# Hybrid encoder, RWKV stage: both directions' chains side by side, outputs summed in PSUM, preparation and filling products dealt between them in fixed order

## The chip, the core and the metric

One Trainium2 chip, one of its cores. A core has TensorE (PE, matrix products; PEld is its weight load), VectorE (DVE), ScalarE (ACT), GpSimd (POOL) and SyncE (SP), which here issues the transfers. Each engine works through a queue of its own and waits on semaphores for the others. The metric is device time in microseconds for one launch; lower is better.

## The reference, cut to what matters

One layer of an encoder on 1024 + 256 tokens of width 1024. An input projection feeds three branches: attention over a neighbourhood of a grid (8 heads), a bidirectional RWKV-7 recurrence (8 heads of 64), and attention over 256 memory tokens (4 heads). Gates merge the branches, then follow an output projection and a feed-forward block. The recurrence is, for each direction d and head:

```python
def step(s, inp):
    r_t, w_t, k_t, v_t, a_t, b_t = inp
    sa = jnp.einsum('bhij,bhj->bhi', s, a_t)
    s = s * w_t[:, :, None, :] + sa[..., None] * b_t[:, :, None, :] + v_t[..., None] * k_t[:, :, None, :]
    return s, jnp.einsum('bhij,bhj->bhi', s, r_t)
...
for d in range(2):
    ...
    ys.append(wkv7_scan(rh, decay, k_d, vh, -kk, kk * a_h, reverse=(d == 1)))
y = ys[0] + ys[1]
```

## The kernel before, in words

Tokens lie along the free dimension. A projection of 128 columns ("block") takes 24 products for each of three token tiles of 512, 512 and 256 columns: 8 slices of the contraction times three (high weight with high input, low with high, high with low), since numbers are split into two parts. `weight_block` loads a block's weights and splits them, ScalarE the high part (`whi`), VectorE the low (`wlo`). `dense_steps` (products on line 205) yields after each 8 products; nine such steps are one block.

The stages follow one another: norms and the RWKV projections; the RWKV stage; attention of grid and memory; merge, output projection, feed-forward. The projections of grid attention (12 blocks), of memory queries (4) and of 20 of the 24 gates are not a stage: they are the **filler**, a generator from which `fill` takes steps while RWKV and attention run.

The RWKV stage (`part_rwkv`) works on 40 items: 4 pairs of heads (p), 5 groups of 256 tokens (s), 2 directions (d). An item has 4 chunks of 64 tokens.

- `rw_prepare` needs nothing of the recurrence's state. It loads k, r and kk (`kr`), makes decays (`th`, `cc`, `E2`), the left matrices `L1` and the keys `BK`, the Gram products `ps_gE` and `ps_gO` (lines 608, 611), their masked forms, and then inverts a triangular 128x128 matrix for each chunk: five doublings of `X` and `XT` (products `ps_y`, line 653, and `ps_x`, line 658; copies on ScalarE, additions and transposes on VectorE, masks `Lk` on POOL), and one correction (`ps_e`, `ps_n`). Result: `TT`, `L3`, `L1`, `R`, `wC`.
- `rw_chain` carries the state through the 4 chunks. For each chunk there are three dependent products, each followed by a copy or sum: `ps_c` from `L1` and `R` (line 707), copied to `Q`; `TT` times `Q` (line 710), copied into `R` by ScalarE and VectorE (lines 719, 720); `L3` times `R` (line 722), from which VectorE makes the next state (731, 732) and the output `Ys` (733, 734, with a part of `Q` added). The tile `ps_c` has one buffer.

Each item is written as: preparation, some filler steps, the chain of the item before, more filler steps. That is only a priority: a scheduler deals instructions to the engines' queues by readiness as it models it. Elsewhere (feed-forward) the kernel pins PE, DVE, ACT and POOL to the written order by `in_order`.

In attention, `grid_attention` runs 80 tiles of 128 queries (scores `ps_s`, softmax, transposes `ps_pt`, output `ps_o`, ended by line 946 on ScalarE), `memory_attention` 20 pairs of tiles; after each of these 100 pieces it takes `self.steps` filler steps. How many is set in lines 844 and 845:

```python
            self.fill(FILL_FIRST)
            self.steps = (9.0 * (16 + RWKV_GATES + ATTENTION_GATES) - self.filled) / 100 * FILL_ATTENTION
```

`self.filled` counts the steps taken since the start of the RWKV stage; FILL_FIRST is 40, FILL_ATTENTION 0.9. `rw_finish` turns the RWKV output round by 64x64 products with the identity (`ps_yt`, line 1058).

Of the kernel before, what the change touches and what calls it, by code (L numbers as in the profile page):

```python
# [30 lines left out]
FILL_PREPARE, FILL_ALL, FILL_FIRST, FILL_ATTENTION = 0.475, 0.955, 40, 0.9  # L31
# [46 lines left out]
def make_consts():  # L78
# [3 lines left out]
    c["ident16"] = np.eye(128, dtype=np.float16)  # L82
    hb = np.arange(128) // 64
# [71 lines left out]
class Builder:  # L155
# [195 lines left out]
    def rwkv_consts(self):  # L351
# [15 lines left out]
        self.ident16 = ld("ident16", [128, 128], F16)  # L367
        d0 = ld("rw_decay0", [128, 2, 4])
# [135 lines left out]
    def part_rwkv(self):  # L504
        nc, tc = self.nc, self.tc
        with ExitStack() as cx:
            pool = cx.enter_context(self.pool("rw", 2))
            self.psg = cx.enter_context(self.pool("psg", 2, space=PSUM))
            self.psl = cx.enter_context(self.pool("psl", 1, space=PSUM))
            self.psi = cx.enter_context(self.pool("psi", 1, space=PSUM))  # L510
            self.psc = cx.enter_context(self.pool("psc", 1, space=PSUM))
            self.L1 = [pool.tile([128, 4, 2, 128], F32, name="L1_%d" % i, bufs=1) for i in range(3)]
            self.LT = [pool.tile([128, 4, 128], F32, name="LT_%d" % i, bufs=1) for i in range(2)]
            for t in self.L1 + self.LT:
                nc.gpsimd.memset(t, 0.0)
            self.item_no = 0
            fwd = [0, 1, 2, 3, 4]
            bwd = [3, 2, 1, 0, 4]
            work = []
            for p in range(4):  # L520
                for i in range(5):
                    work.append((p, 0, fwd[i]))
                    work.append((p, 1, bwd[i]))
            state = {}
            prev = None
            self.filler = chain(self.na_steps(), self.gate_steps(self.st, range(RWKV_GATES + ATTENTION_GATES)))
            self.owed, self.filled = 0.0, 0
            steps = 9.0 * (16 + RWKV_GATES) / len(work)
            for w in work:
                it = self.rw_prepare(pool, *w)  # L530
                self.fill(steps * FILL_PREPARE)
                if prev is not None:
                    self.rw_chain(pool, prev, state)
                self.fill(steps * (FILL_ALL - FILL_PREPARE))
                prev = it
            self.rw_chain(pool, prev, state)

    def rw_prepare(self, pool, p, d, s):

        nc = self.nc  # L540
        i = self.item_no
        self.item_no += 1
        L1, LT = self.L1[i % 3], self.LT[i % 2]
# [4 lines left out]
        kr = tl([128, 3, 256], "kr")  # L548
        nc.sync.dma_start(kr, self.RKV[p][s][:, 0:3, :])
        R = tl([128, 4, 2, 64], "R", bufs=3)  # L550
        nc.sync.dma_start(R, self.VR[p][:, 4 * s:4 * s + 4])

        if d == 0:
            self.lw = tl([128, 2, 256], "lw", bufs=1)
# [1143 lines left out]
```

## Time and profile before

| | |
|---|---|
| median of 3 runs | 3084.71 us (3075.01 to 3108.17) |
| the profiled execution | 3087.64 us, of which its span 3085.9 us |
| mean granted TensorE clock of the span | 0.967 |
| PE / PEld / DVE / ACT / POOL busy | 95% / 80% / 63% / 40% / 35% |
| first to last product of the chains | 391 to 1417 us |
| first transpose of a grid tile to the last of a memory tile | 1473 to 1850 us |

A PE row's duration holds its way through the array, so rows overlap; what one costs in a stream is read from start to start. A 32-bit product is two records, so a count of x4 on `ps_c` is two products. The granted clock is 1.00 at 2.4 GHz and 0.50 at 1.2 GHz.

### The profile page before, as it was taken

The numbers are of one execution on the slowest core, as the hardware profiler recorded it, in microseconds if no ns is written. First come the engines' busy times: TensorE is split into PE (matmuls) and PEld (weight loads), VectorE is DVE, ScalarE is ACT, GpSimd is POOL, SyncE is SP. The second block draws the span as 40 slices with busy tenths as digits, with TensorE's granted clock in tenths as the row PEclk, the third lists the DMA queues.
The fourth block names the chain that finished last, engine by engine and source line by source line (L and its number), as shares of the span: only waits on it lengthen the run. The fifth ranks groups of instructions, "written<-read, shape, count | busy, mean of one in ns | idle before, by whom it ended". The sixth has DMA issues, their size and how long they took to land.

```text
span 3085.9 us, 49265 instructions
## 1 busy us (share of the span) xinstructions
PE 2929.3 (95%) x18164; PEld 2477.7 (80%) x18164; DVE 1946.3 (63%) x4001; ACT 1242.3 (40%) x2693; POOL 1082.5 (35%) x1186
## 2 busy tenths in 40 slices
PE   7999989999999998999989999999899999999999
PEld 6878867767777777777877788898799999997877
DVE  6233387887887888883435551474688888883233
ACT  6322344444444544552545551022244344343232
POOL 2000166765666766662122100000245544441100
PEclk9999988997999999999979999999999999999999
DMA  6332412221222222214546534544112222245343
GB/s 229 119 120 94 137 62 67 73 78 61 76 74 70 86 64 66 66 54 132 167 123 192 178 114 157 191 163 147 66 61 71 75 77 68 68 135 165 131 146 103
DMA packets 212743, 333.51 MB, mean 108 GB/s; under 512 B 45282, under 2 KB 109538, under 8 KB 212502
## 3 DMA queue, kind: packets, MB, share of 16 engines
q1 hardware_dynamic: 211062, 325.12, 32.6%
q10 hardware_dynamic: 1440, 5.24, 0.4%
q8 instruction: 143, 2.34, 0.3%
q14 instruction: 98, 0.80, 0.1%
HBM read 230.15 MB, written 104.07 MB: 108 GB/s over the span
## 4 chain that ended last, share of the span: by engine, by line
PE 75%; DVE 10%; POOL 6%; issue 3%; ACT 3%; DMA 2%; SPq 0%; ACTq 0%; POOLq 0%; DVEq 0%
PE ps_d L205 26%; PE ps_d L1470 16%; PE ps_d L1660 9%; PE ps_w L1167 3%; PE ps_o L945 3%; PE ps_c L722 2%; PE ps_c L707 2%; PE ps_y L653 1%; PE ps_gO L611 1%; PE ps_pt L863 1%; PE ps_x L658 1%; DVE X L661 1%; PE ps_gE L608 1%; PE ps_c L710 1%; PE ps_bt L628 1%
## 5 line engine op out<-in xcount | busy, mean ns | idle before, releaser
L205 PE MATMUL ps_d<-hT,whi 128*128 128x512 f32 (+1 forms) x2688 | 689.3, 381 | 3.5 <-ACT gt L824 2.9
L205 PEld LDWEIGHTS ps_d<-hT,whi 128*128 128x128 f32 x2688 | 450.5, 194 | 65.6 <-issue 5.8
L205 PE MATMUL ps_d<-hT,wlo 128*128 128x512 f32 (+1 forms) x1344 | 358.2, 383 | 0.0
L650 POOL TENSOR_TENSOR Lk<-Lh,c_lev 128x512 f16<-128x512 f16 x200 | 242.2, 1214 | 128.2 <-PE ps_y L653 127.0
L1660 PE MATMUL ps_d<-hT,h2T 128*128 128x512 f32 x1110 | 275.4, 394 | 7.3 <-POOL hT L183 4.1
L1660 PEld LDWEIGHTS ps_d<-hT,h2T 128*128 128x128 f32 x1110 | 210.5, 190 | 54.5 <-POOL hT L183 5.3
L205 PEld LDWEIGHTS ps_d<-hT,wlo 128*128 128x128 f32 x1344 | 229.6, 197 | 29.0 <-issue 2.8
L183 DVE TENSOR_TENSOR wlo<-wraw,whi 128x512 fp32r<-128x512 f32 x152 | 117.1, 781 | 192.9 <-ACT whi L182 192.0
L1374 DVE SCALAR_TENSOR_TENSOR xk<-xk,fconv,xk 128x642 f32<-128x642 f32 (+1 forms) x176 | 178.7, 1026 | 3.1
L655 ACT CAST Yl<-ps_y 128x512 f16<-128x512 f32 x200 | 116.8, 584 | 135.6 <-PE ps_y L653 134.8
L1470 PE MATMUL ps_d<-hT,fwx 128*128 128x256 f32 (+1 forms) x1080 | 159.0, 306 | 2.2 <-ACT fwx L182 1.6
L1470 PEld LDWEIGHTS ps_d<-hT,fwx 128*128 128x128 f32 x1080 | 156.5, 188 | 2.9 <-ACT fwx L182 1.9
L660 ACT CAST X<-ps_x 128x512 f16<-128x512 f32 x200 | 116.7, 584 | 101.7 <-PE ps_x L658 95.2
L1470 PE MATMUL ps_d<-hT,fw 128*128 128x256 f32 (+1 forms) x1032 | 156.1, 310 | 0.6 <-ACT hT L182 0.6
L1340 DVE TENSOR_TENSOR xk<-ps_d,xk 128x256 f32<-128x256 f32 (+1 forms) x308 | 140.6, 480 | 22.1 <-PE ps_d L1470 21.8
L1470 PEld LDWEIGHTS ps_d<-hT,fw 128*128 128x128 f32 x1032 | 153.2, 190 | 1.6 <-ACT hT L182 0.9
L1219 POOL TENSOR_TENSOR xk<-xk 128x1536 f32<-128x1536 f32 (+1 forms) x2 | 5.8, 2918 | 387.2 <-DVE xk L1157 387.2
L182 ACT CAST whi<-wraw 128x512 fp32r<-128x512 f32 x152 | 91.3, 620 | 119.9 <-PE ps_d L205 104.8
L205 PE MATMUL ps_d<-bo,whi 128*128 128x256 f32 (+2 forms) x640 | 127.0, 337 | 4.2 <-DMA bo<-O 3.1
L1383 ACT ACTIVATE xk<-xk 128x320 f32<-128x320 f32 (+1 forms) x88 | 41.7, 474 | 214.9 <-DVE xk L1387 139.8
L707 PEld LDWEIGHTS ps_c<-R,L 128*128 128x128 f32 x640 | 92.0, 201 | 43.2 <-issue 24.8
L1470 PE MATMUL ps_d<-h2T,fw 128*128 128x384 f32 (+1 forms) x840 | 125.4, 308 | 0.0
(353 smaller groups left out, 6437.6 us busy)
## 6 DMA issues: line engine op xcount, KB each, us to landing
wraw<-in_w_in SPq DMA_DIRECT2D x112, 256.0 KB, 2.9
wraw<-in_w_up SPq DMA_DIRECT2D x88, 256.0 KB, 2.6
kr<-RKV SPq DMA_DIRECT2D x40, 384.0 KB, 3.2
bo<-O SPq DMA_DIRECT2D x24, 640.0 KB, 8.7
gate<-GT SPq DMA_DIRECT2D x20, 640.0 KB, 4.0
h2T<-AD SPq DMA_DIRECT2D x17, 704.0 KB, 3.9
h2T<-AD SPq DMA_DIRECT2D x18, 640.0 KB, 5.1
draw<-in_w_down SPq DMA_DIRECT2D x44, 256.0 KB, 2.9
```

Source lines behind the costliest of these rows:

```text
L183: (eng or nc.vector).tensor_sub(lo, src, hi.bitcast(F32))
L205: nc.tensor.matmul(ps[:, :n], lhsT=w[:, k, :], rhs=x[k][:, t0:t0 + n], start=i == 0, stop=i == 3 * kt - 1)
L650: nc.gpsimd.tensor_mul(Lk, Lh, bc(self.lev[:, d, l, :]))
L655: nc.scalar.copy(Yl, py)
L660: nc.scalar.copy(f(X2), f(px))
L707: nc.tensor.matmul(ps[:, 0, h, :], lhsT=L1[:, c, h, :], rhs=R[:, c, h, :], start=True, stop=True)
L945: nc.tensor.matmul(o, lhsT=PT[0:h, j], rhs=V[0:h, k0 // 128 + j, f], start=j == 0, stop=j == nb - 1)
L1167: nc.tensor.matmul(ps[i][:, 512 * f:512 * f + 512], lhsT=self.merged(l, k, 128 * i, 128), rhs=r[:, 512 * f:512 * f + 512], start=k == 0 an ...
L1340: add = lambda o, y: nc.vector.tensor_add(o, ps, y)
L1374: nc.vector.scalar_tensor_tensor(o[:, :m], in0=z[j][:, lo + d:lo + d + m], scalar=fc[:, f + 22 * j, i:i + 1], in1=o[:, :m], op0=ALU.mult, ...
L1470: nc.tensor.matmul(ps, lhsT=w[:, u, 128 * k:128 * k + 128], rhs=B[c][j][v][:, k], start=n == 0, stop=n == 11)
L1660: nc.tensor.matmul(ps[n], lhsT=u, rhs=wd[f][:, v], start=f == 0 and m == 0, stop=f == 21 and m == 2)
```

## The change

- Items go in pairs: chunk group s of the forward and 3-s of the backward direction (the group of the short sequence with itself). `rw_chain` carries both directions at once: 18 products for two chunks (14 where no state goes on) in place of 10, cut to 64x64 output pieces; both outputs are summed over two products each in a PSUM tile `ps_cy`, which ScalarE copies once per pair; the copies to `Q` and `R`, the state's scaling and sums take both directions in one instruction.
- The new state is written straight into the next pair's `R`; the copies through `S`, the zeroing of `R`, and VectorE's sums for `Ys` go.
- In the preparation, `ps_gE` and `ps_gO` alternate; ScalarE's copy of `ps_x` goes (VectorE adds from PSUM); VectorE's two instructions around `ps_e` become two more 16-bit products per chunk and a ScalarE copy.
- `rw_prepare` and `rw_chain` are generators. A loop deals them: 12 chain steps per pair (3 per chunk), between them the 21 steps of both preparations, direction 0 four steps ahead, and 1.5 filler units after each chain step (a unit is 4 products of 512 columns). The whole stage stands in `in_order`.
- `fine_steps` yields after 4 products and loads the next block's weights a block ahead. All 24 blocks that the stage may take are taken in it; twelve gate blocks (108 steps) are left for attention. FILL_FIRST is 30. `self.filled` is set to 0 after the stage; lines 844 and 845 stay (940 and 941 now).

```diff
-FILL_PREPARE, FILL_ALL, FILL_FIRST, FILL_ATTENTION = 0.475, 0.955, 40, 0.9
+FILL_FIRST, FILL_ATTENTION = 30, 0.9
+
+STEPS, HEAD = 21, 4
...
+            with self.in_order():
+                fill = self.fine_steps(self.na_blocks() + self.gate_blocks(self.st, range(RWKV_GATES)))
+                cost = 15.0 * (16 + RWKV_GATES) / (12 * len(work))
+                owed, ahead = 0.0, None
+                for j in range(len(work) + 1):
+                    chain_steps = iter(()) if j == 0 else self.rw_chain(pool, work[j - 1], work[j] if j < len(work) else None)
+                    tokens = []
...
+                        m = STEPS - HEAD
+                        tokens = [x for _ in range(m) for x in (a, b)] + [x for _ in range(HEAD) for x in (b, ahead)]
+                    done = 0
+                    for k in range(12):
+                        next(chain_steps, None)
+                        upto = len(tokens) * (k + 1) // 12
+                        n = max(upto - done, 1)
+                        for _ in range(n):
+                            if done < upto:
+                                next(tokens[done], None)
+                                done += 1
+                            if 0 < j:
+                                owed += cost / n
+                            while owed > 0:
+                                c = next(fill, None)
+                                if c is None:
+                                    break
+                                owed -= c
+                for _ in fill:
+                    pass
+            self.filler = self.gate_steps(self.st, range(RWKV_GATES, RWKV_GATES + ATTENTION_GATES))
             self.owed, self.filled = 0.0, 0
...
             for c in range(4):
                 nc.tensor.matmul(px[:, c, :], lhsT=XT[:, c, :], rhs=Yl[:, c, :], start=True, stop=True)
-            X2 = tl([128, 4, 128], "X%d" % (i % 2), F16, bufs=2)
-            nc.scalar.copy(f(X2), f(px))
-            nc.vector.tensor_add(f(X2), f(X), f(X2))
-            XT2 = tl([128, 4, 128], "XT%d" % (i % 2), F16, bufs=2)
+            X2 = tl([128, 4, 128], "X%d" % d, F16, bufs=2)
+            nc.vector.tensor_add(f(X2), f(X), f(px))
...
+        both = lambda n: slice(n, 8 - n, 7 - 2 * n)
+        for n in range(4):
+            g, cs = both(n), (n, 7 - n)
+            more = n < 3 or not last
             ps = self.psc.tile([128, 3, 2, 64], F32, tag="c", name="ps_c")
...
+            for h, o in enumerate((lo, hi)):
+                for u, c in enumerate(cs):
+                    nc.tensor.matmul(ps[o, 0, u], lhsT=L1[:, c, 2 * h], rhs=R[:, c, h], start=True, stop=True)
+            for u, c in enumerate(cs):
+                for o, q, h in ((lo, hi, 0), (hi, lo, 1)):
+                    nc.tensor.matmul(py[q, u, c - 4 * u], lhsT=L1[o, c, 1], rhs=R[o, c, h],
+                                     start=n == 0 and u == 0, stop=False)
+            Q = pool.tile([128, 2, 64], F32, tag="Q", name="Q", bufs=2)
             nc.scalar.copy(Q, ps[:, 0])
...
+            yield
+
+            for u, c in enumerate(cs):
+                nc.tensor.matmul(ps[:, 1, u], lhsT=TT[u][:, c - 4 * u], rhs=Q[:, u], start=True, stop=True)
+            nc.scalar.copy(R[lo, g, 0], ps[lo, 1])
+            nc.vector.tensor_copy(R[hi, g, 1], ps[hi, 1])
+            yield
+
             if more:
+                for h, o in enumerate((lo, hi)):
+                    for u, c in enumerate(cs):
+                        nc.tensor.matmul(ps[o, 2, u], lhsT=L3[u][:, c - 4 * u, h, o], rhs=R[:, c, h], start=True, stop=True)
+            for u, c in enumerate(cs):
+                for o, q, h in ((lo, hi, 0), (hi, lo, 1)):
+                    nc.tensor.matmul(py[q, u, c - 4 * u], lhsT=L3[u][:, c - 4 * u, h, q], rhs=R[:, c, h],
+                                     start=False, stop=n == 3 and u == 1)
+            if more:
+                dst = R[:, both(n + 1)] if n < 3 else nxt["R"][:, both(0)]
+                for h, o in enumerate((lo, hi)):
+                    nc.vector.tensor_add(dst[o, :, h], SW[o], ps[o, 2])
+            if n == 3:
+                Ys = pool.tile([128, 2, 4, 64], F32, tag="Ys", name="Ys", bufs=1)
+                nc.scalar.copy(Ys, py)
+                for u in range(2):
+                    s = it["s"][u]
+                    nc.sync.dma_start(self.Y[u][p][:, 4 * s:4 * s + 4], Ys[:, u])
+            yield
```

**PE in the chains.** Before, products of one chunk (lines 707, 722) between filler (205) and an inversion's product (658):

```order
L658 MATMUL ps_x<-Yl_11518,XT_11509 128x128
L205 MATMUL ps_d<-hT,whi 128x512 x3
L205 MATMUL ps_d<-hT,whi 128x256
L722 MATMUL ps_c<-R,L_10804 128x64 x2
L205 MATMUL ps_d<-hT,whi 128x256 x7
L205 MATMUL ps_d<-hT,wlo 128x256 x2
L707 MATMUL ps_c<-R,L_1_3023 128x64 x2
L205 MATMUL ps_d<-hT,wlo 128x256
```

Now, the first steps of a pair (750, 753: first products of both directions; 764: `TT`; 914: filler; 576, 577: decays; 644, 646: `ps_gE`, `ps_gO`):

```order
L750 MATMUL ps_c<-R,L_11662 64x64 x4
L753 MATMUL ps_cy<-R,L_11662 64x64 x4
L914 MATMUL ps_d<-hT,whi 128x256 x8
L914 MATMUL ps_d<-hT,wlo 128x256 x4
L764 MATMUL ps_c<-Q,TT 128x64 x2
L576 MATMUL ps_l<-lw,c_rw_decay_407 128x256
L577 MATMUL ps_l<-lw,c_rw_a_409 128x256
L914 MATMUL ps_d<-hT,wlo 128x256 x4
L644 MATMUL ps_gE<-L_12281,BK 128x128
L646 MATMUL ps_gO<-L_12281,BK 128x128
```

Filler stands in whole groups of four between every two steps, and the order is that of the text.

**PE in grid attention.** Before, a tile's scores (927, 928), transposes (863) and outputs (945), with filler (205) throughout:

```order
L927 MATMUL ps_s<-K,Q 128x512
L928 MATMUL ps_s<-KL,Q 128x512
L205 MATMUL ps_d<-hT,whi 128x512 x8
L927 MATMUL ps_s<-K,Q 128x256
L863 MATMUL ps_pt<-c_ident,P 128x128 x4
L928 MATMUL ps_s<-KL,Q 128x256
L927 MATMUL ps_s<-K,Q 128x256
L928 MATMUL ps_s<-KL,Q 128x256
L205 MATMUL ps_d<-hT,whi 128x256
L945 MATMUL ps_o<-V,PT 128x64 x2
L205 MATMUL ps_d<-hT,whi 128x256 x4
```

Now, an early tile (1023, 1024: scores; 959: transposes; 1041: outputs; 208: filler):

```order
L1023 MATMUL ps_s<-K,Q 128x512
L1024 MATMUL ps_s<-KL,Q 128x512
L208 MATMUL ps_d<-hT,whi 128x512 x9
L959 MATMUL ps_pt<-c_ident,P 128x128 x4
L208 MATMUL ps_d<-hT,whi 128x512 x3
L1041 MATMUL ps_o<-V,PT 128x64 x2
L208 MATMUL ps_d<-hT,whi 128x512
L1041 MATMUL ps_o<-V,PT 128x64 x2
```

and a tile of the third pair of heads:

```order
L959 MATMUL ps_pt<-c_ident,P 128x128 x4
L1041 MATMUL ps_o<-V,PT 128x64 x4
L959 MATMUL ps_pt<-c_ident,P 128x128 x4
L1023 MATMUL ps_s<-K,Q 128x512
L1024 MATMUL ps_s<-KL,Q 128x512
L1041 MATMUL ps_o<-V,PT 128x64 x2
L1023 MATMUL ps_s<-K,Q 128x64
L1024 MATMUL ps_s<-KL,Q 128x64
```

From about the sixth tile of the second pair of heads to the end of attention PE's queue holds no filler product at all; ahead of it there are some 21 for each tile.

## Rows read from the trace of the kernel before

**Rows 1.** Stages: length, busy us (count) of PE, PEld, DVE, ACT, POOL; PEclk; DMA
```profile
391.00:1417.00 1026.00, 952.55 (x6757) 744.75 (x6757) 840.93 (x1941) 493.80 (x1212) 653.14 (x863) 0.95 0.21 68
1473.00:1850.00 377.00, 353.30 (x2385) 296.44 (x2385) 188.69 (x599) 194.38 (x542) 59.80 (x43) 0.94 0.54 155
```

**Rows 2.** The same stretches, filler products (line 205) alone: length, PE, PEld, PEclk, DMA
```profile
391.00:1417.00 1026.00, 493.99 (x1662) 276.36 (x1663) 0.95 0.21 68
1473.00:1850.00 377.00, 142.09 (x533) 86.08 (x533) 0.94 0.54 155
```

**Rows 3.** Waits of PE in 391 to 1417: total us, times, longest
```profile
PE ps_y L653 <- DVE X L661: 19.3, 24, 2.3
PE ps_c L722 <- DVE R L720: 16.9, 19, 2.0
PE ps_c L707 <- DVE Ys L734: 12.3, 16, 2.1
```

**Rows 4.** Timeline of PE in the chains: start, us, operation, count
```profile
711.12 0.74 PE L205 MATMUL ps_d<-hT,whi 128*128 128x256 f32 x4
711.79 0.70 PE L558 MATMUL ps_l<-lw,c_rw_decay 64*128 64x256 f32 x2
712.41 0.40 PE L658 MATMUL ps_x<-Yl,XT 128*128 128x128 f16 x4
712.65 0.61 PE L722 MATMUL ps_c<-R,L 128*128 128x64 f32 x4
713.09 0.56 PE L631 MATMUL ps_bt<-rk,rb 128*128 128x2 f32 x4
...
717.13 0.44 PE L710 MATMUL ps_c<-Q,TT 128*128 128x128 f32 x2
717.41 0.39 PE L653 MATMUL ps_y<-X,Lk 128*128 128x128 f16 x4
...
720.05 1.64 PE L205 MATMUL ps_d<-hT,wlo 128*128 128x512 f32 x6
721.52 0.40 PE L205 MATMUL ps_d<-hT,whi 128*128 128x512 f32 x1
...
725.35 0.93 PE L608 MATMUL ps_gE<-L,BK 64*128 64x128 f32 x6
726.31 0.71 PE L611 MATMUL ps_gO<-L,BK 64*128 64x128 f32 x4
```

**Rows 5.** Timeline of PE in attention, around 64x64 products (line 1058)
```profile
1529.22 0.45 PE L1058 MATMUL ps_yt<-c_ident,y 64*64 64x64 f32 x8
1529.60 1.20 PE L978 MATMUL ps_ms<-mk,mq 128*128 128x256 f32 x8
1530.73 1.15 PE L1058 MATMUL ps_yt<-c_ident,y 64*64 64x64 f32 x32
1531.81 1.88 PE L205 MATMUL ps_d<-hT,whi 128*128 128x512 f32 x7
```

**Rows 6.** Groups of VectorE in 391 to 1417, by form: busy us, mean ns
```profile
L661 DVE TENSOR_TENSOR X<-X,X 128x512 f16<-128x512 f16 x200 | 104.3, 522 | 22.5 <-ACT X L660 20.1
L678 DVE TENSOR_TENSOR IX<-IX,ps_e 128x512 f16<-128x512 f16 x40 | 27.3, 682 | 12.5 <-PE ps_e L676 11.9
L733 DVE TENSOR_TENSOR Ys<-Q,ps_c 64x64 f32<-64x64 f32 x159 | 35.4, 222 | 2.1 <-PE ps_c L722 0.9
```

**Rows 7.** Attention stretches without filler, columns as in the first group
```profile
1561.50:1566.00 4.50, 0.00 (x0) 0.00 (x0) 0.00 (x0) 0.38 (x1) 4.50 (x2) 0.85 0.55 166
1573.00:1606.00 33.00, 30.05 (x117) 25.45 (x117) 9.42 (x37) 11.64 (x35) 5.37 (x5) 0.50 0.37 87
1779.00:1797.00 18.00, 14.57 (x99) 12.01 (x98) 7.90 (x33) 10.23 (x30) 3.03 (x4) 1.00 0.55 145
```

**Rows 8.** The same stretches: ends of grid tiles (line 946, one each)
```profile
1573.00:1606.00 33.00, 2.19 (x7) 0.50 0.37 87
1779.00:1797.00 18.00, 1.88 (x6) 1.00 0.55 145
```

More of the change, by code (lines that the diff above doesn't have):

```diff
@@ L508, in part_rwkv @@
             self.psg = cx.enter_context(self.pool("psg", 2, space=PSUM))
[L509 removed]
             self.psi = cx.enter_context(self.pool("psi", 1, space=PSUM))
             self.psc = cx.enter_context(self.pool("psc", 1, space=PSUM))
[L512 removed]
             self.LT = [pool.tile([128, 4, 128], F32, name="LT_%d" % i, bufs=1) for i in range(2)]
[L514 removed]
+            for t in self.LT:
@@ L515, in part_rwkv @@
                 nc.gpsimd.memset(t, 0.0)
[L516 to L526, printed above, removed]
-            self.owed, self.filled = 0.0, 0
@@ L528, in part_rwkv @@
[L528 to L538, printed above, removed]
+            work = [dict(p=p, s=s, i=i, n=5 * p + i, TT=[None] * 2, L3=[None] * 2)
+                    for p in range(4) for i, s in enumerate(((0, 3), (1, 2), (2, 1), (3, 0), (4, 4)))]
@@ new lines, in part_rwkv @@
+            with self.in_order():
[5 more added lines that the diff above has]
+                    tokens = []
+                    if j < len(work):
+                        a = ahead or self.rw_prepare(pool, work[j], 0)
+                        b = self.rw_prepare(pool, work[j], 1)
+                        ahead = self.rw_prepare(pool, work[j + 1], 0) if j + 1 < len(work) else iter(())
+                        if j == 0:
+                            for _ in range(HEAD):
+                                next(a)
+                        m = STEPS - HEAD
[18 more added lines that the diff above has]
+                    pass
@@ L663, in rw_prepare @@
             if l < 5:
                 nc.vector.transpose(f(XT2), f(X2))
-            else:
-                pt = self.psi.tile([128, 4, 128], F16, tag="i%d" % (i % 2), name="ps_xt")
-                for c in range(4):
-                    nc.tensor.transpose(pt[:, c, :], X2[:, c, :], self.ident16)
-                nc.scalar.copy(f(XT2), f(pt))
             X, XT = X2, XT2
-        IX = tl([128, 4, 128], "IX", F16, bufs=1)
-        nc.vector.tensor_sub(IX, bc(self.ident16), X)
-        pe = self.psi.tile([128, 4, 128], F32, tag="i%d" % (i % 2), name="ps_e")
+            yield
@@ new lines, in rw_prepare @@
+        nc.scalar.copy(f(XT), f(pt))
+        yield
+        pe = self.psi.tile([128, 4, 128], F32, tag="i%d" % d, name="ps_e")
+        for c in range(4):
+            for n, (l, r) in enumerate(((self.nident16, X[:, c]), (self.ident16, self.ident16), (Lh[:, c], X[:, c]),
+                                        (Ll[:, c], X[:, c]))):
+                nc.tensor.matmul(pe[:, c, :], lhsT=l, rhs=r, start=n == 0, stop=n == 3)
+        Er = tl([128, 4, 128], "IX", F16, bufs=1)
+        nc.scalar.copy(f(Er), f(pe))
@@ L737, in part_mem_project @@
+            yield
     def part_mem_project(self):
```

215 lines of the change are left out of this document (118 added, 97 removed).

## The prediction

> **What bounds the kernel now.** I first read busy times by stage. From the first to the last product of the chains, 1026 us, PE is busy for 952.6 us and VectorE for 840.9, while POOL has 653.1 and ScalarE 493.8 [rows 1]. So PE is nearly full, VectorE comes next, and nobody else limits. The filler is half of PE's work there [rows 2]. Then I read PE's waits: the three longest groups end on VectorE, 48.5 us together, and one of them is a chain's first product waiting until VectorE has read the `ps_c` of the chunk before for `Ys` [rows 3]. For prices I read PE's timeline from start to start [rows 4, 5]. In attention I looked for stretches without filler, and for the granted clock in them [rows 7, 8].
>
> Per pair of items the chain stage takes 1026 / 20 = 51.3 us. PE is idle in it for (1026 - 952.6) / 20 = 3.7 us. The mean clock is 0.95, and at half clock half the time is lost, so 0.05 of 51.3 = 2.6 us go to the low clock. That leaves 45.0 us of PE work at 2.4 GHz per pair: the stage is bound by PE, with 6.3 us of waits and low clock on top.
>
> **The chain's products.** Before, a chunk takes two products on line 707 and two on 722, 0.44 us for each two (four records), and one on 710, 0.28 us [rows 4]: 1.16 us, 9.3 for a pair's eight chunks. Now two chunks take 18 products: four groups of four on 64-wide pieces (eight records each), and two `TT` products of 64 columns (four records, priced as on line 722 at 0.44). No row has the 64-wide chain product. The nearest is the 64x64 product in attention: eight records take 0.38 us from start to next start, 32 take 1.08 [rows 5], that is 0.147 us for a group and 0.029 for each record. I take that: 4 x 0.38 + 0.44 = 1.96 us for two chunks, 7.8 for a pair, 1.5 less than now. Half of these products contract over 128 rows, unlike that row, so the bounds are wide: with no cost per group 5.5 us, and with each record as dear as one on line 722 (0.11) 15.8 us.
>
> The Trainium skill (TensorEngine Tiling (Array Packing), Theoretical Speedup) gives up to a factor of two for each dimension of at most 64. By it a group of eight would take a quarter of 0.88, 0.22 us, and the pair 5.3. The trace does not agree: its group of eight takes 0.38, so the rule is kept only as a small rival.
>
> **The preparation's products.** The correction gets two more 16-bit products per chunk, 16 per pair at 0.24 / 4 = 0.06 us [rows 4]: +1.0 us. `ps_gE` and `ps_gO` have 32 records per pair at 0.96 / 6 = 0.16 us, 5.1 us. They now alternate between the upper and lower half of the contraction rows. That could save nothing, or half if the halves overlapped; no row shows the alternation, and since the 64x64 products of both halves in [rows 5] do come cheaper than full ones I take a quarter, -1.3.
>
> **The filler in the stage.** 1662 products now, 83.1 per pair; then all 24 blocks of 72, 86.4 per pair. One of 512 columns takes 1.47 / 6 = 0.245 us, one of 256 takes 0.67 / 4 = 0.168 [rows 2, 4]; a block has two of the first to one of the second, mean 0.219. So +0.7 us.
>
> PE work per pair becomes 45.0 - 1.5 + 1.0 - 1.3 + 0.7 = 43.9 us: hardly less than now. What the change can win are the 6.3 us beside it.
>
> **Waits and clock.** VectorE does 840.9 / 20 = 42.0 us per pair. It loses 16 `Ys` sums at 0.22 and four instructions around `ps_e` at 0.68 or a little less [rows 6], -3.5 and -2.6. Copies and sums for two directions at once halve 22 instructions of about 0.22, which then are longer; I count -1.7. The ten additions from PSUM cost 0.68 in place of 0.52 [rows 6], +1.6. That makes 35.8, or 10 us of slack in 46. The wait for `Ys`, 12.3 / 20 = 0.6 us [rows 3], cannot come back, since outputs no longer leave `ps_c`. A filler group between every two steps covers waits of about a microsecond and keeps long stretches of small products from forming. I keep a third of the 6.3, 2.1 us, so a pair takes **46.0 us**. The bounds are 43.9 (no wait left) and 52.7 (below).
>
> The stage is then 19 x 46.0, and for the last pair, which has no preparation beside it, 18.9 of filler + 7.8: 901 us, 125 less. Against it stands the start: the first chain now waits for both items and gets no filler beside it. VectorE has about 20 us for an item; I count half of it as exposed, +10. **The chain stage: -115 us.** Loads move ahead by a block or a step on SP's queue; DMA is busy for 0.21 there [rows 1], so they cost nothing. If that cover failed, it would be `kr`, now with one buffer for both items, that is late, and two steps lie between its load and its use.
>
> **Attention.** Here the change does something that its loop does not show. Line 845 divides what is left by 100 pieces after taking off `self.filled`. Before, that is 206 steps of the RWKV stage plus 40, so 0.70 steps per piece. Now the count restarts at 0 after the stage: (324 - 30) / 100 x 0.9 = 2.65 steps per piece, with only 108 - 30 = 78 left. They are gone after 30 of 100 pieces, as the order of PE shows. The other seventy run bare.
>
> What a bare tile costs, two stretches tell. In 33 us at clock 0.50 seven tiles ended, 4.7 us each; in 18 us at clock 1.00 six tiles, 3.0 us each [rows 7, 8]. The whole stretch of attention, less its 533 fillers x 0.219 = 117 us, has (377 - 117) / 100 = 2.6 us per piece [rows 1, 2], so a bare piece is 0.4 us longer than its work. The sum at full clock: +28 for seventy pieces, +12 for three passages from one pair of heads to the next where filler covered loads (four microseconds each, an estimate; between nothing and ten), +20 since 624 fillers stand here, not 533, -3 for 12 fewer ahead, -14 for the eight steps that came after the last piece, and -17 because the one cold stretch shown (seven tiles x 1.7, and 5 us of standing still before it) is filled now. **+26 us.**
>
> Then the clock. It fell in a stretch of 4.5 us in which PE did nothing, and stayed at 1.2 GHz through the bare tiles although PE was busy for 30 of 33 us; in the other bare stretch it stayed at 2.4 GHz [rows 7]. A pair of heads at the low clock costs 20 tiles x 1.7 = 34 and about 11 for its memory part: 45 us. The last two pairs of heads, and their passages, are wholly bare. I take one of the two: **+71 us**.
>
> **The forecast.** The profiled execution took 3087.6 us, 2.9 above the median. 3087.6 - 115 + 71 = **3044 us**.
>
> **The rivals.**
>
> - *The clock holds in attention.* The passages stay short, and nothing falls: +26 in place of +71, 2998 us. For it: the 18 us at full clock. Against: the 33.
> - *Both last pairs of heads run at the low clock*: +116, 3089 us, no change. For it: once low, it did not rise again without filler.
> - *The fixed order holds PE up.* Place: the first five of a pair's twelve steps, where both items' masks of `ps_gE` and `ps_gO` stand on VectorE, and the next transposes need their two PSUM buffers. Behind a product that waits, all filler waits too. Price: four waits per pair of the longest kind seen, 2.2 us [rows 3], so 52.7 us per pair, 19 x 52.7 + 27 + 10 - 1026 = +12, and 3170 us with attention's +71. It decides from 48.3 us per pair, where the two stages cancel. For it: VectorE already releases PE's longest waits, and now no scheduler moves other work ahead. Against: VectorE gets 6 us less to do. The Trainium skill (TensorE: Matmul & The Clock Gate, Step-by-step: what each phase is for) says that matmuls stay in program order and only weight loads are pulled ahead; [rows 3] agrees in that PE has such waits at all.
> - *Small products cost as much as full ones*: 15.8 for 7.8 us, 54.0 per pair, 3196 us. The price in [rows 5] speaks against it.
> - *Small products overlap wholly*: 5.3 us, 2.5 less, 19 x 2.5 = 48, 2996 us.
>
> **How the numbers follow.** Chances: forecast 0.35, clock holds 0.17, both low 0.18, order holds PE up 0.22, small products dear 0.05, wholly overlapping 0.03. The forecast's own range is 3000 to 3085, from a pair at 44 to 48 us. The range of 8 in 10 reaches from 2975 (clock holds, pair a microsecond better) to 3150, and leaves out the upper half of the held-up case and the dear products. This kernel's measurement cannot tell less than 1%, 31 us, from no change. Below 3054 lie six tenths of the forecast (0.21), the holding clock (0.16), a sixth of the both-low case (0.03) and the overlap (0.03): 0.43 faster. Above 3116 lie most of the held-up case (0.18), the dear products, and bits of the forecast and the both-low case (0.06): 0.29. The rest, 0.28, is no change.
>
> **What would show it.** Chains: the time from first to last chain product near 900 us, granted clock above 0.97, waits of PE for VectorE below those now, groups of eight small records at about 0.38 us. Attention: no row of filler after a third of it, tiles at 3.0 or 4.7 us, with the granted clock beside them. I am wrong if PE's waits per pair stay above 4 us, if the small products cost over 0.6 us per group, or if bare tiles come faster than 2.6 us.

## The result, and the profile after

The change made the kernel slower: 3208.69 us (median of 4 runs, 3194.18 to 3223.2) against 3085.08 of the kernel before on the same chip, ratio 1.039, 95% interval 1.031 to 1.047. Forecast were 3044 us, with a range from 2975 to 3150. The profiled execution took 3199.98 us, its span 3198.2, 112.3 more than before.

Stages of the kernel after: first product of the preparation to first product with `TT`; chains; passage; attention. Columns as in [rows 1].

```profile
378.00:434.00 56.00, 35.07 (x222) 26.75 (x222) 36.59 (x58) 18.02 (x37) 33.24 (x37) 0.53 0.10 29
434.00:1427.00 993.00, 871.78 (x8146) 684.10 (x8145) 717.40 (x1255) 385.61 (x863) 559.14 (x667) 0.93 0.22 72
1427.00:1482.00 55.00, 53.65 (x287) 45.59 (x286) 15.60 (x24) 16.38 (x29) 16.75 (x9) 1.00 0.65 192
1482.00:1962.00 480.00, 419.63 (x2475) 346.64 (x2474) 197.08 (x604) 200.97 (x551) 60.08 (x43) 0.85 0.43 124
```

The first two stretches of the kernel before, cut in the same way:

```profile
378.00:427.00 49.00, 42.35 (x252) 31.61 (x250) 38.80 (x62) 22.71 (x50) 36.16 (x44) 0.83 0.28 98
427.00:1417.00 990.00, 919.47 (x6547) 719.74 (x6547) 809.48 (x1891) 475.42 (x1172) 626.50 (x835) 0.95 0.21 69
```

I cut at the first product with `TT`, because the 391 us of [rows 1] mark only a first `ps_c` that the scheduler had pulled ahead; the chains ran from 427. From there on they took 990 us before and 993 after, where the forecast took more than 100 us off. PE did lose work: before, 919.5 us busy at clock 0.95 are 870 us at full clock, after, 871.8 at 0.93 are 802, so 43.5 became 40.1 us per pair. But idle time went from 3.5 to 6.1 us per pair, and the low clock (0.07 of 49.7 in place of 0.05 of 49.5) from 2.5 to 3.5. What PE gained in work it lost again in waits and clock, in the same stage. Attention, the same stretch as in [rows 1], takes 480 us in place of 377. The ends add up: chains +10, passage -1, attention +103.

Waits of PE in the chains after (total us, times, longest), which answer to [rows 3]:

```profile
PE ps_gE L644 <- DVE BK L631: 30.9, 31, 1.4
PE ps_bt L681 <- DVE L L659: 28.6, 34, 1.1
PE ps_bt L684 <- ACT L L682: 18.3, 38, 0.7
PE ps_y L694 <- DVE X L705: 13.2, 30, 1.3
```

The wait on `Ys` is gone, as foreseen. In its place stand two waits for most of the 40 items: for the keys `BK` (31 times), and for the buffer that the masks of `ps_gE` still read (34 times). PE's timeline shows one item's passage, in fixed order (start, us, operation, count, idle time before):

```profile
810.85 1.17 PE L914 MATMUL ps_d<-hT,whi 128*128 128x512 f32 x4
812.18 0.38 PE L694 MATMUL ps_y<-X,Lk 128*128 128x128 f16 x4 [0.15 <-DVE X L705]
813.84 0.37 PE L644 MATMUL ps_gE<-L,BK 64*128 64x128 f32 x1 [1.27 <-DVE BK L631]
813.84 0.37 PE L646 MATMUL ps_gO<-L,BK 64*128 64x128 f32 x1
814.05 0.27 PE L644 MATMUL ps_gE<-L,BK 64*128 64x128 f32 x1
814.06 0.27 PE L646 MATMUL ps_gO<-L,BK 64*128 64x128 f32 x1
...
814.93 0.66 PE L764 MATMUL ps_c<-Q,TT 128*128 128x64 f32 x4
815.42 0.39 PE L703 MATMUL ps_x<-Yl,XT 128*128 128x128 f16 x4
815.62 0.72 PE L914 MATMUL ps_d<-hT,whi 128*128 128x256 f32 x4
817.28 0.88 PE L681 MATMUL ps_bt<-c_ident,BD 64*128 64x64 f32 x8 [0.94 <-DVE L L659]
818.62 0.61 PE L684 MATMUL ps_bt<-rk,rb 128*128 128x2 f32 x4 [0.46 <-ACT L L682]
819.09 0.72 PE L914 MATMUL ps_d<-hT,whi 128*128 128x256 f32 x4
```

Filler (line 914) stands on both sides of the waits, and in the fixed order the filler behind a waiting product may not go ahead of it. The same place in slices of 2 us, columns as above:

```profile
812.00:814.00 2.00, 0.57 (x7) 0.37 (x7) 1.75 (x4) 1.17 (x2) 0.84 (x4) 1.00 0.45 124
814.00:816.00 2.00, 2.00 (x27) 1.88 (x28) 0.91 (x3) 0.06 (x1) 2.00 (x2) 1.00 0.87 303
816.00:818.00 2.00, 1.04 (x11) 0.76 (x10) 1.89 (x6) 0.97 (x3) 1.88 (x3) 1.00 0.08 32
818.00:820.00 2.00, 1.54 (x15) 1.35 (x14) 1.93 (x4) 0.66 (x3) 0.90 (x1) 0.92 0.03 8
820.00:822.00 2.00, 2.00 (x23) 1.78 (x20) 0.95 (x3) 0.59 (x1) 1.15 (x1) 0.50 0.00 0
```

PE is idle for 2.9 of the first eight microseconds. In the three slices where it stands still VectorE (third busy column) works almost without pause, and the slice after them runs at 1.2 GHz. The pair shown has two such dips, one for each item (the other at 806 to 808 us, clock 0.51).

Attention after, in stretches:

```profile
1482.00:1680.00 198.00, 191.33 (x1157) 159.06 (x1156) 69.07 (x187) 73.60 (x190) 24.69 (x18) 0.98 0.47 137
1680.00:1730.00 50.00, 40.83 (x330) 33.31 (x330) 24.91 (x92) 26.97 (x81) 3.05 (x4) 1.00 0.46 124
1730.00:1760.00 30.00, 19.98 (x89) 15.05 (x89) 20.14 (x47) 14.35 (x34) 8.48 (x4) 0.80 0.80 225
1760.00:1840.00 80.00, 74.02 (x291) 63.01 (x290) 24.11 (x95) 29.00 (x83) 10.34 (x10) 0.50 0.31 79
1840.00:1890.00 50.00, 34.22 (x218) 27.04 (x218) 25.45 (x70) 22.20 (x57) 13.52 (x8) 0.76 0.58 174
1890.00:1920.00 30.00, 24.89 (x170) 20.92 (x168) 13.40 (x56) 16.77 (x51) 0.00 (x0) 1.00 0.06 23
1920.00:1962.00 42.00, 34.34 (x231) 28.25 (x231) 20.00 (x62) 18.08 (x56) 0.00 (x0) 0.76 0.25 92
```

All 612 filler records here lie before 1680. The third pair of heads' grid tiles run at 1.2 GHz, though PE is busy for 74 of 80 us. Of the two passages from one pair of heads to the next, 1730 to 1760 and 1840 to 1890, and of the end the means lie between the two levels.

### The profile page after: what moved, and what is told of

Read it like the earlier page. It is cut to its first block, busy times and chain, and to the rows that moved or that the text cites. A ratio compares the mean times of both kernels' runs of the same rounds, so it can differ in the third digit from the quotient of the medians.

```text
span 3198.2 us, 50945 instructions
## 1 busy us (share of the span) xinstructions
PE 2923.4 (91%) x19700; PEld 2470.5 (77%) x19700; DVE 1854.0 (58%) x3353; ACT 1150.5 (36%) x2369; POOL 1009.6 (32%) x1007
## 4 chain that ended last, share of the span: by engine, by line
PE 64%; DVE 13%; ACT 3%; issue 3%; POOL 2%; DMA 1%; SPq 0%; ACTq 0%; DVEq 0%; POOLq 0%
PE ps_d L1566 16%; PE ps_d L208 11%; PE ps_d L1756 9%; PE ps_d L914 8%; PE ps_o L1041 3%; PE ps_w L1263 3%; DVE X L705 1%; PE ps_pt L959 1%; PE ps_y L694 1%; PE ps_x L703 1%; PE ps_gE L644 1%; PE ps_e L723 1%; DVE XT L708 1%; DVE L L621 1%; DVE wlo L186 1%
## 5 line engine op out<-in xcount | busy, mean ns | idle before, releaser
L208 PE MATMUL ps_d<-hT,whi 128*128 128x512 f32 (+1 forms) x1536 | 341.1, 366 | 7.1 <-ACT whi L185 5.8
L914 PE MATMUL ps_d<-hT,whi 128*128 128x512 f32 (+1 forms) x1152 | 313.1, 400 | 0.3 <-ACT whi L185 0.3
L208 PEld LDWEIGHTS ps_d<-hT,whi 128*128 128x128 f32 x1536 | 259.3, 193 | 50.7 <-ACT whi L185 6.6
L914 PEld LDWEIGHTS ps_d<-hT,whi 128*128 128x128 f32 x1152 | 199.4, 206 | 29.4 <-issue 5.0
L705 DVE TENSOR_TENSOR X<-X,ps_x 128x512 f16<-128x512 f16 x200 | 134.8, 680 | 86.2 <-PE ps_x L703 84.1
L208 PE MATMUL ps_d<-hT,wlo 128*128 128x512 f32 (+1 forms) x768 | 172.3, 362 | 0.0
L914 PE MATMUL ps_d<-hT,wlo 128*128 128x512 f32 (+1 forms) x576 | 159.8, 403 | 0.0
L208 PEld LDWEIGHTS ps_d<-hT,wlo 128*128 128x128 f32 x768 | 130.2, 192 | 20.1 <-issue 0.3
L1041 PEld LDWEIGHTS ps_o<-V,PT 128*128 128x128 f32 (+1 forms) x640 | 108.8, 231 | 45.7 <-ACT PT L963 18.6
L1041 PE MATMUL ps_o<-V,PT 128*128 128x64 f32 (+1 forms) x640 | 118.8, 319 | 20.9 <-ACT PT L963 9.6
```

The costliest lines, as they stand in the source:

```text
L208: nc.tensor.matmul(ps[:, :n], lhsT=w[:, k, :], rhs=x[k][:, t0:t0 + n], start=i == 0, stop=i == 3 * kt - 1)
L705: nc.vector.tensor_add(f(X2), f(X), f(px))
L914: nc.tensor.matmul(ps[:, :n], lhsT=w[:, k, :], rhs=x[k][:, t0:t0 + n], start=j == 0 and k == 0, stop=j == 2 and k == 7)
L1041: nc.tensor.matmul(o, lhsT=PT[0:h, j], rhs=V[0:h, k0 // 128 + j, f], start=j == 0, stop=j == nb - 1)
```

## The experiments

Times are medians, ratios are to the kernel before in the same session. Chains: first product with `TT` to last chain product. Attention: first `ps_pt` to last `ps_mt`. Both are read from one profiled execution, whose whole time lies up to 19 us off the median (e2), so differences of a few microseconds between them mean nothing.

| kernel | us | ratio (95%) | chains | attention |
|---|---|---|---|---|
| before | 3083 to 3098 | 1 | 427 to 1417 | 377 |
| after | 3208.7 | 1.039 (1.031 to 1.047) | 434 to 1427 | 480 |
| e1 filler spread | 3086.6 | 0.999 (0.996 to 1.002) | 437 to 1423 | 376 |
| e2 before, filler early | 3200.7 | 1.036 (1.030 to 1.042) | 432 to 1428 | 462 |
| e3 after, free order | 3136.5 | 1.016 (1.008 to 1.024) | 423 to 1338 | 497 |
| e4 spread, filler at start | 3103.6 | 1.005 (1.002 to 1.008) | 438 to 1438 | 383 |
| e5 spread, free order | 2995.6 | 0.971 (0.968 to 0.974) | 425 to 1332 | 359 |
| e6 spread, PE free | 3076.0 | 0.996 (0.994 to 0.998) | 436 to 1420 | 373 |
| e7 spread, PE alone fixed | 3118.6 | 1.009 (1.005 to 1.012) | 439 to 1463 | 362 |
| e8 spread, two empty steps | 3092.1 | 1.001 (0.998 to 1.003) | 437 to 1429 | 369 |
| e9 spread, staggered | 3090.1 | 1.000 (0.997 to 1.003) | 446 to 1423 | 368 |
| e10 spread, no alternation | 3101.4 | 1.004 (1.002 to 1.007) | 436 to 1437 | 366 |
| e11 e5, staggered | 3021.0 | 0.979 (0.974 to 0.983) | 431 to 1358 | 373 |
| e12 spread, filler loose | 3048.8 | 0.982 (0.975 to 0.989) | 429 to 1348 | 430 |
| e13 spread, chains loose | 3082.3 | 0.995 (0.993 to 0.998) | 427 to 1421 | 363 |
| e14 e12, attention's held back | 3016.7 | 0.974 (0.970 to 0.977) | 428 to 1350 | 373 |
| e15 e14, filler in its pair | 3062.6 | 0.994 (0.990 to 0.997) | 433 to 1388 | 361 |
| e16 e14, filler in two pairs | 3050.7 | 0.991 (0.988 to 0.993) | 434 to 1390 | 368 |

**Attention's filler (e1, e2).** In e1 the count carries on from the chain stage; e2 deals 2.65 steps per piece in the kernel before.

```diff
-            self.owed, self.filled = 0.0, 0
+            self.owed, self.filled = 0.0, 9 * (16 + RWKV_GATES)
```

```diff
-            self.steps = (9.0 * ...
+            self.steps = 3.77 * (9.0 * ...
```

> The changed kernel with one number altered: after the chain stage the count of filler steps is set to 216 in place of 0, so that the later stage deals 0.70 steps per attention piece again, as before the change. Theory 1: nearly the whole loss is the filler that attention uses up too early, some 103 us between its first and last tile, and nothing else makes up for it; so about 3105 us (3090 to 3120), filler in attention to its end, and the chain stage unchanged at 998 us. Rival: attention loses its time to the new chain stage in other ways (transfers or buffers that come later), and the filler only moves it; then 3155 us or more.

> The kernel before with one number altered: each attention piece is followed by 2.65 filler steps in place of 0.70, the total the same, so that filler is gone after about 30 of 100 pieces. Theory 1 (early filler is what attention pays for): about 3185 us, 100 more than before, with the granted clock at 0.50 in at least one pair of heads. Rival (the loss needs the new chain stage): under 3130 us.

122 us went with one number, and 109 came with one in the kernel before, which has nothing else of the change. The restart of the count alone is the loss in attention; what is left of the change gains nothing and costs nothing (0.999). Two details were missed: e1 came out 3 us below the range given for it, and in e2 the clock fell in many short stretches (mean 0.79 from 1680 us on, where its filler was used up), not through a whole pair of heads.

**The fixed order (e3, e5).** The order is left out, on the kernel after and on the spread one.

```diff
-            with self.in_order():
+            if True:
                 fill = self.fine_steps(...
```

> The changed kernel without the fixed order in the chain stage: each engine's instructions there are put in order by the scheduler, all else the same. Theory 2 (the fixed order holds TensorE up behind waiting products, while filler stands behind them): waits go back to about 4 us per pair and the stage from 998 to some 945 us, the whole to about 3155. Rival (VectorE's own sequence is late, whoever orders TensorE): the stage stays at 990 us or grows, the whole 3200 us or more.

> The changed kernel with both alterations of before: attention filler at 0.70 steps per piece, and the scheduler in place of the fixed order in the chain stage. The two losses lie in different stages, so the gains should add: 3087 for the spread kernel, less the 72 us that the free order gave, about 3015 us, which beats the kernel before by 2 per cent. Rival: with its attention repaired, the 45 us that the chain stage gained by the free order come back as a later attention (filler or loads that the scheduler puts elsewhere); then 3050 us or more.

In e3 (two runs) the chains end 89 us sooner, more than expected, and attention again pays for its early filler. Without either fault (e5) the change beats the kernel before by 2.9%, 19 us more than the two gains added up to. In e5 the chains and attention read:

```profile
425.00:1332.00 907.00, 857.27 (x8011) 650.43 (x8011) 717.76 (x1245) 369.04 (x852) 562.35 (x664) 0.96 0.23 74
1387.00:1746.00 359.00, 340.84 (x2417) 286.69 (x2416) 194.48 (x600) 195.34 (x546) 60.24 (x43) 1.00 0.56 163
```

and the longest waits of PE in its chains:

```profile
PE ps_bt L681 <- DVE L L659: 12.5, 18, 2.1
PE ps_c L764 <- DVE TT L732: 7.3, 13, 1.4
```

VectorE does the same 717 us of work as in the kernel after, in 86 us less; the wait for `BK` is no longer among the first. Part of these 86 us is that 39 us of filler (163 products) now run ahead of the stretch, before 425 us; in the kernel after these were 4 us (8 products).

**Which engine's order (e6, e7).** The list of engines that `in_order` binds is cut (e7: to PE alone).

```diff
-            with self.in_order():
+            with self.in_order([e for e in IN_ORDER if e != mybir.EngineType.PE]):
```

> The spread kernel with the fixed order kept on VectorE, ScalarE and POOL, and TensorE alone left to the scheduler. Theory 2a (what hurts is TensorE's order: filler stands behind waiting products): most of the free order's gain comes, 3020 to 3035 us, with the chain stage at 945 to 955 us. Theory 2b (what hurts is that VectorE takes up the next item's work too late in the dealt order): TensorE's freedom is of little use, 3070 us or more, the stage above 980.

> The mirror image: the spread kernel with the fixed order kept on TensorE alone, and VectorE, ScalarE and POOL left to the scheduler. Theory 2a: the stage stays near 991 us, the whole near 3085. Theory 2b: VectorE comes earlier to what TensorE waits for, the waits of ps_gE shrink to a fifth, and the whole comes to 3020 to 3040 us.

Both theories fell in the form I gave them. Freeing PE takes 0.3% off e1, which the intervals do not tell from nothing; freeing the other three makes it 1% slower. Either half of the order is enough to hold up the whole.

**Distance between steps (e8, e9, e11).** e8 adds a step after `BD` (shown) and one after the masks; e9 changes HEAD (shown) and the buffers for it: `R` is loaded with the second direction, `L3` has five buffers and `Q` one, and two small tiles share the buffer of `th`. e11 is e9 without the fixed order.

```diff
-STEPS, HEAD = 21, 4
+STEPS, HEAD = 23, 4
...
         yield
+        yield
```

```diff
-STEPS, HEAD = 21, 4
+STEPS, HEAD = 21, 9
```

> The spread kernel, its fixed order kept on all engines, with two empty steps more in each preparation: one between VectorE's product BK and the ps_gE that reads it, one between the masks of ps_gE and ps_gO and the transposes into the buffers they free. At each place a step of the other direction and its filler come between. If the two longest waits are a matter of distance in the dealt order, they go from some 60 us to under 20 and the two dips of the clock per pair with them: stage 991 to about 930, the whole about 3025 us. If VectorE is simply late by its whole sequence, the waits turn up at the next steps (ps_bt, ps_y) and the time stays within 15 us of 3087.

> The spread kernel in its fixed order, with the next item's first direction nine steps ahead of the other in place of four, so that the heavy VectorE steps of the two directions (the products before ps_gE and the masks behind it) lie 9 and 12 steps apart in the dealt order and not in one run; buffers are rearranged for it (R loaded with the second direction, L3 with five buffers, two small tiles placed in th, Q with one buffer). If the waits come from VectorE's bunched steps in the first third of a pair, they fall by half, the stage goes from 991 to about 945 us and the whole to about 3040. If the fixed order costs because every engine stands behind its own waiting instruction wherever the steps are dealt (as the moved waits of the kernel with two empty steps suggest), the waits only move again and the whole stays within 15 us of 3087.

> The same wider distance between the two directions, with the scheduler in place of the fixed order. If the scheduler already spreads VectorE's heavy steps by itself, the time stays within 10 us of the 2996 of the free and spread kernel. If bunching still costs there (10.6 us of the waits of ps_bt and ps_gE on VectorE's masks and sums remain), some 15 us less, 2980.

The waits moved and the time stayed. In e8's chains the old places shrank (`ps_gE` is not among the longest any more) and the next ones grew:

```profile
PE ps_y L696 <- DVE X L671: 35.5, 21, 3.5
PE ps_y L696 <- DVE X L707: 23.4, 28, 1.1
PE ps_y L696 <- POOL Lk L675: 17.0, 12, 2.2
```

In e9 it is `BK` again:

```profile
PE ps_gE L645 <- DVE BK L632: 61.3, 37, 3.0
```

So distance in the dealt order is not enough: e8 shows it with nothing else changed. e9 alone does not settle it, because its buffers changed too: in free order the same edits (e11) were slower than e5 by 25 us, which neither expectation had, and a gain of that size could be hidden in e9. Why e11 is slower is open; in it VectorE's `BK` waits 12.4 us for a tile of POOL's that now shares a buffer, in e5 3.3.

**Which work must be free (e12 to e16).** `in_order` gets a set of instructions to leave out: in e12 the filler with its splits and evacuations, in e13 the chains.

```diff
+                                at = len(code())
                                 c = next(fill, None)
+                                loose.update(id(i) for i in list(code())[at:])
```

> The spread kernel, where the fixed order on all four engines holds only chains and preparation; the filling products with their weight splits and evacuations are left to the scheduler. If the price of the fixed order is that filler stands behind waiting instructions on TensorE, and its splits and evacuations behind waiting ones on ScalarE and VectorE (so that freeing TensorE alone could not help), nearly all of the free order's gain comes: stage end near 1340 us, the whole 2995 to 3020. If it is the order among preparation and chains, the whole stays above 3065.

> The mirror image: preparation and filler in the fixed order, the chain's instructions on all four engines left to the scheduler. If filler locked in the order is the price, it stays here, and the whole is 3065 us or more. If the chain's steps, dealt at even distances, hold up the rest, most of the gain comes here: 3020 or less.

Loose filler brings the end of the chains from 1423 to 1348 us, loose chains to 1421. It is the filler. But the scheduler now ran it whenever PE was free: 50 us before the chains, the rest of the stage's own up to about 1115 us, then 129 us of attention's inside the stage. Attention, left with too little, ran in part at the low clock, as in the kernel after, and so the whole missed its 2995 to 3020:

```profile
429.00:1349.00 920.00, 886.41 (x8446) 694.44 (x8446) 717.14 (x1264) 387.18 (x885) 578.72 (x673) 0.98 0.25 81
1393.00:1822.00 429.00, 385.39 (x2079) 322.00 (x2079) 180.94 (x590) 187.52 (x523) 59.65 (x43) 0.70 0.44 124
```

The filler products of the chain stage, in e1 and then in e12 (ahead of the stage, the stage's own in it, attention's in it), columns as in [rows 2]:

```profile
437.00:1423.00 986.00, 460.06 (x1709) 291.17 (x1708) 0.94 0.23 73
300.00:429.00 129.00, 49.64 (x209) 34.38 (x209) 0.97 0.34 113
429.00:1348.00 919.00, 390.13 (x1519) 242.31 (x1519) 0.98 0.25 81
429.00:1348.00 919.00, 129.15 (x478) 77.46 (x478) 0.98 0.25 81
```

So e12's stage is shorter although it holds more filler, 1997 products in place of 1709.

e14 forbids attention's first 30 steps on PE before the last fixed instruction of the stage (`end`); e15 and e16 bind also each pair's filler behind the end of the pair ahead, or of the one before that, in the same way.

```diff
             self.fill(FILL_FIRST)
+            for i in list(bb.bb.instructions)[at:]:
+                if i.engine == mybir.EngineType.PE:
+                    self.tc.add_manual_dep(i, end, ...
```

> The kernel with loose filler, in which the scheduler put more than half of attention's filler into the end of the chain stage (filler gone in half of attention, clock 0.70 there), with one bond more: attention's first 30 filler steps may not come on TensorE before the last instruction of the chains. If early filler is again what attention pays for, attention goes from 430 back to some 365 us; the chain stage keeps its own filler alone, which ends at about 1115 us, and the rest of it runs bare. If the bare chains keep the pace they have beside filler, the whole comes to 2980 us or less; if they run at 1.2 GHz as attention's bare pieces did, the stage gets no shorter than 1348 and the whole is about 2990 to 3010.

> Fixed order for chains and preparation, loose filler, attention's first 30 steps held back as before, and each pair's filler may not come on TensorE before the last product of the pair ahead of it, so that the stage's filler lasts to its end. If the loose filler's loss is only that it is used up by 1115 us, TensorE's 40 us of work per pair run with waits and low clock of some 3 us beside them: stage 860 to 880 us in place of 922, the whole about 2965. If filler bound to its pair again stands behind waits there, the stage is 907 us or more, and the whole is 2996 or more.

> As the kernel that binds each pair's filler to its pair, but the bond lies one pair further back: filler may come up to a whole pair early. If room to move is what filler needs, this is the faster of the two by some 10 us, about 2955; if a pair's own room is enough, the two are within 5 us of each other.

e14 repairs attention (373 us), as expected, comes out at 3017 us where at most 3010 were expected, and shows the chains with and without filler:

```profile
430.00:800.00 370.00, 355.90 (x3358) 278.87 (x3358) 298.22 (x526) 156.69 (x357) 238.56 (x276) 0.98 0.28 90
800.00:1000.00 200.00, 193.86 (x1891) 152.31 (x1888) 156.54 (x275) 87.62 (x199) 125.34 (x148) 0.99 0.25 82
1000.00:1100.00 100.00, 96.16 (x917) 75.66 (x917) 77.99 (x137) 42.12 (x99) 66.61 (x77) 1.00 0.25 79
1100.00:1200.00 100.00, 77.55 (x717) 62.34 (x715) 73.14 (x131) 37.00 (x85) 61.07 (x74) 0.71 0.17 54
1200.00:1330.00 130.00, 96.71 (x930) 79.34 (x931) 94.88 (x170) 46.01 (x106) 80.08 (x96) 0.63 0.09 27
```

Up to 1100 us loose filler keeps PE busy for 96% at clock 0.98 to 1.00. From then on there is none, the clock falls to 0.63, and VectorE does no more per microsecond (0.73) than beside filler (0.78 to 0.81): bare chains are no faster. Binding the filler to its pair (e15, e16) makes it last to the end of the chains, but gives back half of what these had gained and two thirds or more of the whole gain; the 2965 and 2955 us forecast for them were far off. What the bond takes is not one thing: in e14 209 of the filler's products ran before the first product with `TT`, in e15 8, in e16 86, so that part of e14's lead is filler that ran before the chains. e16 was faster than e15 by 12 us in the median, about what more room was to bring, but the intervals overlap. The scheduler's own deal (e5) stays the best tried.

**Alternating halves (e10).** The four products of `ps_gE` come first, then those of `ps_gO`.

```diff
             nc.tensor.matmul(gE[...
+        for c in range(4):
             nc.tensor.matmul(gO[...
```

> The spread kernel with the eight products of each ps_gE and ps_gO pair in the old order, the four of ps_gE first and then the four of ps_gO, all else and the order of everything else the same. If alternating between upper and lower contraction rows makes them overlap, the eight products go from about 1.1 us to 2.4 from first to last, 40 times over 1.3 us: the stage 40 to 55 us longer, the whole about 3135. If the gain was not theirs, the stage stays within 10 us of 991 and the whole near 3087.

The chains end 14 us later, between the two expectations. The timeline says why:

```profile
801.33 0.82 PE L644 MATMUL ps_gE<-L,BK 64*128 64x128 f32 x5 [0.89 <-DVE BK L631]
801.88 0.37 PE L647 MATMUL ps_gO<-L,BK 64*128 64x128 f32 x1
801.99 0.27 PE L644 MATMUL ps_gE<-L,BK 64*128 64x128 f32 x1
...
802.21 0.27 PE L644 MATMUL ps_gE<-L,BK 64*128 64x128 f32 x1
802.32 0.72 PE L647 MATMUL ps_gO<-L,BK 64*128 64x128 f32 x5
802.97 1.19 PE L915 MATMUL ps_d<-hT,wlo 128*128 128x512 f32 x4
```

From first to next product the sixteen records take 1.64 us; alternated, in the kernel after, 1.09 (813.84 to 814.93). The medians over the 38 items that the traces hold nearly whole are 1.64 and 1.10. Forty times 0.55 are 22 us, of which 14 show.

**Filler at the start (e4).** It is dealt also while the first pair is prepared, a 21st part of it in each step.

```diff
-                            if 0 < j:
-                                owed += cost / n
+                            owed += cost / n
```

> The kernel with spread attention filler, and filler also dealt beside the first pair's preparation, where no chain runs yet (each step then gets a 21st part of the stage's filler instead of a 20th). Theory 3: TensorE is idle for 14 of the first pair's 37 us at a low clock, and 17 us of filler fit there; the stage that follows loses as much filler and gets shorter, so about 15 us less than the spread kernel. Rival: the chains' pace is set by waits and not by the amount of filler, then the time stays within 5 us of the spread kernel's.

It gained nothing and lost 17 us, a loss that neither expectation had; the chains end 15 us later, with more waits on `ps_y` (33 us in place of 20). Filler bound into the order is not free even where PE seems idle.

## Why the prediction was wrong

**The step that failed** is "I keep a third of the 6.3, 2.1 us", with the sentence before it, that filler between every two steps covers waits of about a microsecond. Measured: 9.6 us per pair, 6.1 idle and 3.5 by the low clock. A place in the order covers a wait only with what stands ahead of the waiting product; what stands behind it waits too, as PE's timeline shows. That it was the filler's place that cost is shown by e12, with chains and preparation still in fixed order: PE is idle for 34 of 920 us at clock 0.98, in the kernel after for 121 of 993 at 0.93, and loose chains (e13) bring nothing. e6 and e7 show that freeing one side does not do; that on the other side the filler's splits and evacuations stand behind waits on ScalarE and VectorE I infer from e6 beside e12, no run frees them alone. This was my rival of the fixed order, which I gave 0.22. Its place was half right: the buffers behind the masks, not the wait for `BK`. Its threshold of 48.3 us per pair was passed (49.7). Its 8.8 us of waits came near the 9.6, but by luck: the waits were 6.1, and the low clock that made up the rest was not in it. Its 52.7 us was too high because PE's work fell further than I thought. Against it I had set that VectorE would get less to do. It did (35.9 us per pair, forecast 35.8), but VectorE's slack is of no use to a product that waits for one certain instruction of it.

**PE's work** fell by 3.4 us per pair, forecast 1.1. The alternated products take 1.09 us per item by the passage shown, in place of 2.56 by [rows 4]. Over the whole stages, from start to start, without idle time and with the low clock in it, their lines fell from 4.55 to 2.44 us per pair, -2.1 where I took -1.3 (some of their records are missing in both traces). Counted in the same way, the chains' products fell from 10.2 to 7.8 us, -2.4 where I took -1.5. The groups of eight small records come at 0.28 to 0.39 us (0.38 forecast). Filler and correction were about as priced (+0.6 for +0.7, +0.7 for +1.0).

**Attention** had the right mechanism and too small a size: +103 for +71. Per pair of heads at the low clock I had 45 us; the rows lose 40 at clock 0.50, but 28 more in the passages and at the end, where I had let the clock hold; that is 23 of the 32 us. From the whole stretches before and after, of the 103 us the low clock makes 49 (72 in place of 23), PE's idle time 37, and its work 17. Bare tiles took 3.1 us at clock 1.00 (16 in 50 us) and 4.4 at 0.50 (18 in 80), forecast 3.0 and 4.7.

**The start** cost +7 us to the first product with `TT`, forecast +10. The stage's sum held an error from the stretch that I had chosen as well: I had put the 36 us before that product (391 to 427) into the mean per pair, 45.0 us of work where 43.5 is right.

Not settled: why the kernel with the wider distance is slower in free order (e11), and whether a fixed order with better dealt filler could beat the scheduler.

## What to carry to other kernels

Before trusting a counter that deals out filling work, follow it through the whole program: the same steps dealt early cost more than 100 us, because PE waits more in the bare rest and falls to the low clock. A fixed order binds the filler as well. Leave the filler loose and look where the scheduler then puts it, or check for each wait what stands ahead of it: moving steps apart moved the waits here and saved no time. And a saving of work on the bounding engine is worth nothing until one has seen that the waits beside it do not grow.

## What the runs showed of the hardware

Products that contract over 64 rows, alternating between the upper and lower half, overlap almost wholly: sixteen records in 1.09 us, against 0.16 us each (2.56) in [rows 4]. The two records of a pair start within 0.01 us of each other (814.05, 814.06), and the pairs follow at 0.11 us, no slower than the five records of one half in e10 (0.55 us from 801.33 to 801.88). The Trainium skill (TensorEngine Tiling (Array Packing), Theoretical Speedup) gives up to a factor of two where a dimension is at most 64; the ratio here is 2.3 against [rows 4], whose records stand among other products, and 1.5 against e10.

In e10 the first `ps_gO` record starts (801.88) before the last of the `ps_gE` records ahead of it in the program (802.21): by the records, products of the two halves do not start in program order. The same holds in 33 of the 38 items that e10's trace holds whole. The Trainium skill (TensorE: Matmul & The Clock Gate, The mechanism) says that products start and end in order; these records differ from it.

In the kernel after PE was busy for 5.2 of the 8 us ahead of the slice at 0.50 (812 to 820), while in e14 it stayed at 0.98 to 1.00 for 670 us beside loose filler, and bare attention held 1.00 from 1890 to 1920 with PE busy for 25 of 30 us.
